# A 31-tap convolution beside projections: GpSimd's taps taken as products from ScalarE, twelve of them, and layer 0's mask and sinks loaded in the projection code

## Chip, cores and metric

One core of a Trainium2 chip. The metric is device microseconds of one execution; the kernel before has 3096.5 us, the median of three runs (3095.42 to 3097.85).

## What is computed

A backbone of two layers over 1024 latent tokens and 256 context tokens of width 1024. The change lies in layer 0. From the normalized, modulated input `h` one projection gives a gated pair for a convolution (2 x 512 columns), queries (512), keys and values (128 each):

```
def conformer_conv(z, conv_w, conv_b, ln_g, ln_b):
    val, gate = z[..., :CONV_A_DIM], z[..., CONV_A_DIM:]
    u = val * jax.nn.sigmoid(gate)
    u = dwconv(u, conv_w, conv_b, half, half)          # 31 taps per channel, 512 channels
    u = layer_norm(u, ln_g, ln_b)
    return jax.nn.silu(u)
...
    s_lat = jnp.where(valid[None, :, None, None], s_lat, NEG_INF)       # the window's mask
    sink_l = sink.astype(jnp.float32).reshape(1, 1, kvh, g, 1, 1)
    p_lat, p_ctx, _ = joint_softmax([s_lat, s_ctx, sink_l])
```

The convolution and the windowed attention stand side by side; their outputs are joined and projected.

## The kernel before

Activations lie with channels on partitions and tokens along the free axis, in groups of 512, 512 and 256 tokens (`TOK`). Every product is made three times, with a high and a low part of weight and input (`gemm`, L315 to L317, on TensorE); its result lies in one of four PSUM banks (`bank`, tile `mm`) until ACT or DVE evicts it. A weight block (`wcol`) is loaded by SP, its high part cast on ACT (L295) and its low part subtracted on DVE or POOL (L298).

At the start x and the context are loaded by SP (L570), transposed by PE (L579), copied out of PSUM by DVE and ACT in turn (L580), squared on ACT (L469) and summed on POOL (L473). From these sums come the root mean squares (L436 to L457), from the modulation vectors (L358, L345, L350, L411) the normalized input (L496 to L503), and then the first projection. Parameters go by small loads that ACT issues (L270); a tile `par` holds four groups of them until PE transposes each (L274).

`proj0` walks the list `PROJ0 = g0 g1 q0 g2 q1 g3 k q23`. `glu(i)` projects gate and value of channel block i and forms a tile `u` of 1325 columns in SBUF; it then spawns `conv(i, U)`, a generator that is advanced while later projections are written down (`pump`). `conv` takes tap 15 with the bias on ACT into `ca`, which lies in PSUM (L638); the first 8 other taps (`PTAPS`) on POOL, each as a product into a buffer `cp` (L645) and an addition of the sum so far (L647); the other 22 on DVE as multiply-adds into `ca` (L650). DVE joins both sums in `co` (L653), and SP writes that out. `qproj` projects queries (L780), `kvproj` keys and values (L706 evicts the values, L321 splits the keys, L709 and L710 rotate them). Beside them `mods` makes modulation vectors in the background: PE multiplies (L369), ACT copies the result `t` (L345), PE transposes it (L350), DVE adds the bias (L411). Then the queries' rotations (`qstack`, L746 to L762) and the values' transposes (`vstack`, L731).

`attn0` follows. It takes PSUM's banks of `ca` for the scores (`big`), loads mask and sink on ACT's queue (L801, L803) and negates the sink on DVE (L805). Scores are L861 and L868, the mask and the maximum L873, the exponential L878, the transposes of the weights L906.

What order the instructions of an engine stand in is set by a scheduler from the code's priorities and its own estimates, not by the code's order alone; on each engine they then run in that order. A DMA also waits until the load before it on its lane (there are eight) has landed.

Of the kernel before, what the change touches and what calls it, by code (L numbers as in the profile page):

```python
# [11 lines left out]
F32 = mybir.dt.float32  # L12
F32R = mybir.dt.float32r
AF = mybir.ActivationFunctionType
ALU = mybir.AluOpType
# [26 lines left out]
YF = 6.0  # L42
O0 = "G"
MS = ((0, 5), (1, 1), (1, 0), (1, 2), (1, 4), (1, 3), (1, 5)), ()
PTAPS = 8
WS = {"p0": P0W, "o0": O0, "f0": "GV", "c0": "GV", "p1": "GV", "m1": "G", "o1": "V", "f1": "G"}
PB0 = 4
LAG0 = 3
# [50 lines left out]
def tile_backbone(ctx: ExitStack, tc: tile.TileContext, a: dict, out: bass.AP):  # L99
    nc = tc.nc  # L100
    V, S, G, T = nc.vector, nc.scalar, nc.gpsimd, nc.tensor
# [21 lines left out]
    def nm(s):  # L123
        uid[0] += 1
        return f"{s}{uid[0]}"
# [135 lines left out]
    for r, items in enumerate(rows):  # L261
        n = 0
# [343 lines left out]
    CW, UW = SEQ + 15 + CTX, SEQ + 15 + CTX + 30  # L606
    COFF = (0, 512, SEQ + 15)

    def mixer0(hs, nxt, xs0):
        w = a["ab_w_in"][0]  # L610
        pc = ph[0]
        rcos, rsin = pc.tile([128, 1024], F32, name="rcos", bufs=1), pc.tile([128, 1024], F32, name="rsin", bufs=1)
        protr = pc.tile([128, 3, 128], F32R, name="protr", bufs=1)
        with tc.tile_pool(name="m0a", bufs=1) as pa:
            prep = proj0(hs, w, pa, rcos, rsin, protr, xs0)
        psum_side("big", 2)
        cat = Lazy()
        with tc.tile_pool(name="m0b", bufs=1) as pb:
            attn0(pb, *prep, cat)
        ws[0] = "o0"  # L620
        with tc.tile_pool(name="m0o", bufs=8 * len(YPO)) as po:
            for i, g in enumerate(GO0):
                if i < 2:
                    spawn(cat.load(GO0[i + 1]), "cat")
                ys, sq, last = outproj(a["ab_w_out"][0], cat, g, (lambda g: [po.tile([128, 512], F32, tag="y", name=nm("y")) for _ in range(8)]) if g in YPO else (lambda g: acts(g, 8, F32, "y")), lambda g: PO0[g], range(7, -1, -1) if g in OR0 else None)
                drain("cat")
                spawn(update(0, g, ys, sq, 2, last, True, (0, 3, 4) if g < 2 else None, nxt, PU0[g]))
            pumping[0] = True
            while not posted >= {(0, g) for g in YPO}:
                advance(flows["norm"])  # L630
            pumping[0] = False

    def proj0(hs, w, pa, rcos, rsin, protr, xs0):
        def conv(i, U):
            wc = lambda k: cols("acw", k * 4 + i)
            A = wide()[:, 0:CW]
            B = None
            S.activation(A, U[:, 15:15 + CW], AF.Identity, scale=wc(15), bias=cols("acb", i))  # L638
            taps = [k for k in range(31) if k != 15]
            pt, dt = taps[:PTAPS], taps[PTAPS:]  # L640
            nch = 6
            for c in range(nch):
                for k in pt[c::nch]:
                    P = pa.tile([128, CW], F32, tag="cp", name=nm("cp"), bufs=2)
                    G.tensor_scalar(P, U[:, k:k + CW], wc(k), 1.0, ALU.mult, ALU.mult)  # L645
                    if B is not None:
                        G.tensor_add(P, P, B)  # L647
                    B = P
                for k in dt[c::nch]:
                    V.scalar_tensor_tensor(A, U[:, k:k + CW], wc(k), A, ALU.mult, ALU.add)  # L650
                yield CY
            O = pa.tile([128, CW], F32, tag="co", name=nm("co"), bufs=2)
            V.tensor_add(O, A, B)  # L653
            for g in range(3):
                nc.sync.dma_start(cd[g][:, i], O[:, COFF[g]:COFF[g] + TOK[g]])

        st = pa.tile([128, CW], F32, tag="cp", name=nm("par"), bufs=2)
        for r in range(1, 5):
            spawn(params(r, st[:, r * 128 - 128:r * 128]), "par")

# [29 lines left out]
        def kvproj():  # L690
            prot = tmp(384).rearrange("p (a b) -> p a b", a=3)
            nc.scalar.dma_start(prot, a["rot"])
            V.tensor_copy(protr, prot)
            wk, wv = wcol(w, 1536), wcol(w, 1664)
            for g in range(3):
                n = TOK[g]
                ps = bank()[:, 0:n]
                gemm(ps, wk, *hs[g])
                if g < 2:
                    kh, kl = tmp(dt=F32R), tmp(dt=F32R)  # L700
                    split(ps, kh, kl)
                else:
                    V.tensor_copy(KFC[:, 0], ps)
                p2 = bank()[:, 0:n]
                gemm(p2, wv, *hs[g])
                S.copy(VF[:, OFF[g]:OFF[g] + n] if g < 2 else KFC[:, 1], p2)  # L706
                if g < 2:
                    pp = bank()
                    T.matmul(pp, protr[:, 0], kh, start=True, stop=False)  # L709
                    T.matmul(pp, protr[:, 0], kl, start=False, stop=True)  # L710
                    dst, m2 = KF[:, OFF[g]:OFF[g] + n], tmp()
                    V.tensor_mul(dst, ps, rcos[:, OFF[g]:OFF[g] + n])
                    V.tensor_mul(m2, pp, rsin[:, OFF[g]:OFF[g] + n])
                    V.tensor_add(dst, dst, m2)
# [50 lines left out]
        KH, qs = [], {}  # L765
# [30 lines left out]
        drain("bg")  # L796
        return KH[0:2], KH[2], vstack, kstack, qstack, qs

    def attn0(pc, KH, KC, vstack, kstack, qstack, qs, cat):
        msk = pc.tile([128, 1152], F32, name="msk")  # L800
        nc.scalar.dma_start(msk, a["win_mask"])  # L801
        sink = pc.tile([128, 8], F32, name="sink")
        nc.scalar.dma_start(sink, a["b_sink"].to_broadcast([128, 8]))  # L803
        nsink = pc.tile([128, 8], F32, name="nsink")
        V.tensor_scalar_mul(nsink, sink, -1.0)  # L805

        cath, catl = [[], [], []], [[], [], []]

# [38 lines left out]
        def scores(i, b, RAW, ROT, res):  # L847
            kv = i // 2
            pair = pc.tile([128, 1282], F32, tag="p", name=nm("p"), bufs=PB0).rearrange("p (j n) -> p j n", j=2)
            mx = pc.tile([128, 2], F32, tag="mx", name=nm("mx"), bufs=4)  # L850
            nmx = pc.tile([128, 2], F32, tag="nmx", name=nm("nmx"), bufs=4)
            den = pc.tile([128, 2], F32, tag="den", name=nm("den"), bufs=4)
            ss = []
            for j in range(2):
                s = bank2()
                if b < 8:
                    k0, k1 = max(0, b - 1), min(8, b + 2)
                    nw = 128 * (k1 - k0)
                    kt = list(range(k0, k1)) + [8, 9]
                    for x in range(2):  # L860
                        T.matmul(s[:, 512 - nw:512], ROT[j][:, b * 128:b * 128 + 128], KH[kv][x][:, k0 * 128:k1 * 128], start=x == 0, stop=x == 1)  # L861
                    q = RAW[j][0][:, b * 128:b * 128 + 128]
                    mk = msk[:, 0:640] if 0 < b < 7 else (msk[:, 128:640] if b == 0 else msk[:, 640:1152])
                else:
                    nw, kt, mk = 0, [8, 9], msk[:, 384:640]
                    q = RAW[j][1][:, (b - 8) * 128:(b - 8) * 128 + 128]
                for x in range(2):
                    T.matmul(s[:, 512:768], q, KC[:, kv, x], start=x == 0, stop=x == 1)  # L868
                n = nw + 256
                if j == 0:  # L870
                    gcopy(pair[:, :, n], sink[:, 2 * i:2 * i + 2])
                    res += [[pair[:, j] for j in range(2)], kt]
                V.tensor_tensor_reduce(out=pair[:, j, 0:n], in0=s[:, 512 - nw:768], in1=mk, op0=ALU.add, op1=ALU.max, scale=1.0, scalar=-3.0e38, accum_out=mx[:, j:j + 1])  # L873
                if j:
                    V.scalar_tensor_tensor(nmx, mx, -1.0, nsink[:, 2 * i:2 * i + 2], ALU.mult, ALU.min)
                yield
            for j in range(2):
                S.activation(pair[:, j, 0:n + 1], pair[:, j, 0:n + 1], AF.Exp, bias=nmx[:, j:j + 1], accum_out=den[:, j:j + 1])  # L878
                yield
            V.reciprocal(den, den)  # L880
            for j in range(2):
                norm1(N0[j], pair[:, j, 0:n], pair[:, j, 0:n], den[:, j:j + 1])
# [329 lines left out]
    def mla(pc, tab, KR, wv):  # L1212
# [163 lines left out]
        def head(h, g):  # L1376
            qh, ql, qc = (x[:, OFF[g]:OFF[g] + 512] for x in Q[h])
            kh, kl, kc = K[h % NK]
            po = psum["po"].tile([128, 512], F32, tag="po", name=nm("po"))
            P = []  # L1380

            def pv(t):
                v = VA[:, t, h // 2, h % 2:h % 2 + 2].rearrange("p b m -> p (b m)")
                T.matmul(po, v, P[t], start=t == 0, stop=t == 9)  # L1384

            for t in range(10):
# [13 lines left out]
                S.activation(p, st, AF.Exp, scale=scale)  # L1400
                P.append(p)
                if t % 2 and t > PVD:
# [298 lines left out]
    hs, nxt = Lazy(), Lazy()  # L1701
# [125 lines left out]
```

## Time and profile before

| | |
|---|---|
| median of three runs | 3096.5 us (3095.42 to 3097.85) |
| the profiled execution | 3100.69 us, its span 3098.9 us |
| mean granted TensorE clock | 0.974 of full speed |
| PE busy | 2942.0 us (95%) |
| DVE, ACT, POOL busy | 1747.0, 1093.4 and 990.6 us (56%, 35%, 32%) |

The span is what the trace shows; the execution's own time is 1.8 us longer, and that execution 4.2 us above the median. Busy shares are means over stages that differ: in layer 0's projections DVE and POOL are busy much more than over the span, so the stage is to be read by itself.

### The profile page before, as it was taken

To read this page: it belongs to the slowest core of one execution; us is meant where nothing else is said; L and a number is where in the kernel's file an instruction comes from. 1 tells how busy PE (TensorE), PEld (TensorE's weight loads), DVE (VectorE), ACT (ScalarE), POOL (GpSimd) and SP (SyncE) were. 2 spreads that over 40 slices of the span, in tenths; PEclk is the share of its full clock that TensorE was granted. 3 is DMA by queue.
4 is the path that set the end of the run, shared out by engine and by line. 5 is a ranking of instruction groups with operands and counts; after the bars stand their busy time and mean duration, and the time that the engine had idled before them with its cause. 6 is when DMAs were issued, how large, how long until landed. Compare 5 with 4: busy or idle time off the path is not lost. (4 is left out here: it accounts for less than half of the span.)

```text
span 3098.9 us, 37481 instructions
## 1 busy us (share of the span) xinstructions
PE 2942.0 (95%) x14441; PEld 2356.5 (76%) x14441; DVE 1747.0 (56%) x2631; ACT 1093.4 (35%) x1631; POOL 990.6 (32%) x730
## 2 busy tenths in 40 slices
PE   7997899899999999999999889999998999999998
PEld 4886777778888888889997556666686888888886
DVE  4799883665654455568545986667355132232234
ACT  4213884532221112145433763333344222111213
POOL 4676546821110011055432341110253222112223
PEclk8998999999999999999999899999998999999999
DMA  8343113434442344269744230010152121111212
GB/s 295 119 129 100 37 34 111 147 101 129 139 136 82 116 144 145 88 195 281 246 155 152 94 111 26 31 38 28 57 160 89 48 62 55 34 41 55 61 41 109
DMA packets 330768, 327.04 MB, mean 106 GB/s; under 512 B 27121, under 2 KB 280734, under 8 KB 330590
## 3 DMA queue, kind: packets, MB, share of 16 engines
q1 hardware_dynamic: 326784, 321.74, 32.3%
q10 hardware_dynamic: 3806, 2.91, 0.3%
q8 instruction: 113, 1.85, 0.2%
q14 instruction: 65, 0.53, 0.1%
HBM read 255.36 MB, written 69.21 MB: 105 GB/s over the span
## 5 line engine op out<-in xcount | busy, mean ns | idle before, releaser
L298 POOL TENSOR_TENSOR wl<-wr,wh 128x1024 fp32r<-128x1024 f32 x154 | 379.9, 2468 | 1314.2 <-ACT wh L295 1283.1
L295 ACT CAST wh<-wr 128x1024 fp32r<-128x1024 f32 x248 | 259.9, 1049 | 1072.3 <-PE big L316 682.3
L315 PE MATMUL big<-hh,wh 128*128 128x512 f32 x1376 | 541.2, 394 | 4.9 <-DVE ga L1485 2.6
L316 PE MATMUL big<-hl,wh 128*128 128x512 f32 x1376 | 538.6, 392 | 3.1 <-POOL hl L503 3.1
L317 PE MATMUL big<-hh,wl 128*128 128x512 f32 x1376 | 538.8, 392 | 0.6 <-DVE wl L298 0.6
L315 PE MATMUL mm<-hh,wh 128*128 128x256 f32 (+1 forms) x1000 | 346.0, 346 | 9.6 <-DVE i L1031 9.5
L316 PE MATMUL mm<-hl,wh 128*128 128x256 f32 (+1 forms) x1000 | 339.0, 339 | 4.0 <-POOL hl L503 2.0
L317 PE MATMUL mm<-hh,wl 128*128 128x256 f32 (+1 forms) x1000 | 338.0, 338 | 3.2 <-POOL wl L298 2.5
L315 PEld LDWEIGHTS big<-hh,wh 128*128 128x128 f32 x1376 | 260.7, 190 | 61.9 <-ACT hh L498 3.4
L316 PEld LDWEIGHTS big<-hl,wh 128*128 128x128 f32 x1376 | 260.4, 189 | 58.9 <-POOL hl L503 4.3
L317 PEld LDWEIGHTS big<-hh,wl 128*128 128x128 f32 x1376 | 260.5, 189 | 55.6 <-DVE wl L298 1.0
L1553 PE MATMUL mm<-zh,wh 128*128 128x512 f32 x704 | 276.6, 393 | 1.2 <-ACT xt L1656 0.7
L1554 PE MATMUL mm<-zl,wh 128*128 128x512 f32 x704 | 275.0, 391 | 0.3 <-DVE zl L322 0.3
L1555 PE MATMUL mm<-zh,wl 128*128 128x512 f32 x704 | 275.2, 391 | 0.0
L1560 DVE TENSOR_TENSOR acc<-acc,mm 128x512 f32<-128x512 f32 x224 | 150.5, 684 | 178.7 <-PE mm L1555 178.5
L473 POOL TENSOR_TENSOR sq<-t,sq 128x512 f32<-128x512 f32 (+1 forms) x153 | 194.8, 1276 | 170.2 <-ACT t L469 152.0
L1485 DVE SCALAR_TENSOR_TENSOR ga<-big,C,ga 128x1023 f32<-128x1023 f32 x86 | 110.2, 1281 | 235.1 <-ACT ga L1498 233.8
L315 PEld LDWEIGHTS mm<-hh,wh 128*128 128x128 f32 x1000 | 192.3, 192 | 35.7 <-DVE i L1031 9.9
L316 PEld LDWEIGHTS mm<-hl,wh 128*128 128x128 f32 x1000 | 191.9, 192 | 29.4 <-POOL hl L503 5.0
L317 PEld LDWEIGHTS mm<-hh,wl 128*128 128x128 f32 x1000 | 191.6, 192 | 24.3 <-POOL wl L298 3.3
L398 DVE SCALAR_TENSOR_TENSOR wa<-wm,sc,wa 128x256 f32<-128x256 f32 x280 | 148.9, 556 | 90.4 <-DMA wm<-in_w_mod_dram 87.6
L298 DVE TENSOR_TENSOR wl<-wr,wh 128x1024 fp32r<-128x1024 f32 x94 | 131.5, 1399 | 111.6 <-ACT wh L295 108.6
(350 smaller groups left out, 5278.5 us busy)
## 6 DMA issues: line engine op xcount, KB each, us to landing
wr<-in_ffn_w_up_dram SPq DMA_DIRECT2D x132, 512.0 KB, 4.3
wm<-in_w_mod_dram SPq DMA_DIRECT2D x224, 128.0 KB, 2.2
wr<-in_ffn_w_down_dram SPq DMA_DIRECT2D x44, 512.0 KB, 3.5
wm<-in_w_mod_dram SPq DMA_DIRECT2D x40, 512.0 KB, 6.5
xd<-x SPq DMA_DIRECT2D x38, 512.0 KB, 4.1
x<-xd SPq DMA_DIRECT2D x38, 512.0 KB, 6.6
wr<-in_ab_w_out_dram SPq DMA_DIRECT2D x24, 512.0 KB, 7.2
wdd<-wh SPq DMA_DIRECT2D x22, 512.0 KB, 2.6
```

What stands on the lines that cost most here:

```text
L295: S.copy(hi[:, 0:nk, 0:m], raw[:, 0:nk, 0:m])
L298: (G if e[wn[0] % len(e)] == "G" else V).tensor_sub(lo[:, 0:nk, 0:m], raw[:, 0:nk, 0:m], f32(hi[:, 0:nk, 0:m]))
L315: T.matmul(ps, wh, xh[k], start=i == 0, stop=False)
L316: T.matmul(ps, wh, xl[k], start=False, stop=False)
L317: T.matmul(ps, wl, xh[k], start=False, stop=i == n - 1)
L398: V.scalar_tensor_tensor(acc[:, v], raw, sc[:, k, v:v + 1], acc[:, v], ALU.mult, ALU.add)
L473: self.eng.tensor_add(self.acc[-1], t, self.acc[-1])
L1485: V.scalar_tensor_tensor(dst[:, lo:hi], src[:, lo + d - o:hi + d - o], k, dst[:, lo:hi], ALU.mult, ALU.add)
L1553: T.matmul(ps, wh, zh, start=j == j0, stop=False)
L1554: T.matmul(ps, wh, zl, start=False, stop=False)
L1555: T.matmul(ps, wl, zh, start=False, stop=j == j1 - 1)
L1560: V.tensor_add(ys[g][c], ys[g][c], ps)
```

## The change

The tap products move from POOL (`G.tensor_scalar`) to ACT (`S.mul`), POOL keeps the additions, and there are 12 such taps a block instead of 8, so DVE has 18 instead of 22. `cp` has three buffers instead of two, `co` one instead of two. The mask's first 640 columns, the sink and its negative get tiles that outlive the projections, and their loads stand in `kvproj`'s code; the last 512 columns (`msk7`) are loaded in `attn0`.

```diff
-PTAPS = 8
+PTAPS = 12
...
+        masks = [pc.tile([128, n], F32, name=s_, bufs=1) for s_, n in (("msk", 640), ("sink", 8), ("nsink", 8))]
...
-                    P = pa.tile([128, CW], F32, tag="cp", name=nm("cp"), bufs=2)
-                    G.tensor_scalar(P, U[:, k:k + CW], wc(k), 1.0, ALU.mult, ALU.mult)
+                    P = pa.tile([128, CW], F32, tag="cp", name=nm("cp"), bufs=3)
+                    S.mul(P, U[:, k:k + CW], wc(k))
                     if B is not None:
                         G.tensor_add(P, P, B)
...
-            O = pa.tile([128, CW], F32, tag="co", name=nm("co"), bufs=2)
+            O = pa.tile([128, CW], F32, tag="co", name=nm("co"), bufs=1)
...
-        st = pa.tile([128, CW], F32, tag="cp", name=nm("par"), bufs=2)
+        st = pa.tile([128, CW], F32, tag="cp", name=nm("par"), bufs=3)
...
             nc.scalar.dma_start(prot, a["rot"])
+            nc.scalar.dma_start(masks[0], a["win_mask"][:, 0:640])
+            nc.scalar.dma_start(masks[1], a["b_sink"].to_broadcast([128, 8]))
+            V.tensor_scalar_mul(masks[2], masks[1], -1.0)
...
-        msk = pc.tile([128, 1152], F32, name="msk")
-        nc.scalar.dma_start(msk, a["win_mask"])
-        sink = pc.tile([128, 8], F32, name="sink")
-        nc.scalar.dma_start(sink, a["b_sink"].to_broadcast([128, 8]))
-        nsink = pc.tile([128, 8], F32, name="nsink")
-        V.tensor_scalar_mul(nsink, sink, -1.0)
+        msk, sink, nsink = masks
+        msk7 = pc.tile([128, 512], F32, name="msk7")
+        nc.scalar.dma_start(msk7, a["win_mask"][:, 640:1152])
...
-                    mk = msk[:, 0:640] if 0 < b < 7 else (msk[:, 128:640] if b == 0 else msk[:, 640:1152])
+                    mk = msk[:, 0:640] if 0 < b < 7 else (msk[:, 128:640] if b == 0 else msk7)
```

With the change the lines below L611 have numbers higher by 1 to 4: the products are L646, the additions L648, the multiply-adds L651, `co` L654, the gate's eviction L676, the value's L710.

PE's order is the same but for some instructions at the first scores. The other engines' orders differ up to the first part of the attention and are the same behind it. Three places follow.

At the program's start, on ACT, behind the parameters' loads; `x` are the copies of the transposed input. Before:

```order
L270 DMA par_645<-in_ffn_conv_w_dram 66x128
L270 DMA par_645<-in_ffn_conv_b_dram 22x128
L580 COPY x_157<-mm_169 128x512
L580 COPY x_158<-mm_187 128x512
L469 ACTIVATE sq_167<-x_157 128x512
```

and with the change:

```order
L270 DMA par_648<-in_ffn_conv_w_dram 66x128
L270 DMA par_648<-in_ffn_conv_b_dram 22x128
L694 DMA msk<-in_win_mask_dram 128x640
L695 DMA sink<-in_b_sink_dram 128x8
L580 COPY x_157<-mm_169 128x512
L580 COPY x_158<-mm_187 128x512
L469 ACTIVATE sq_167<-x_157 128x512
```

The loads of mask and sink stand here, ahead of ACT's first copy of x. On DVE, at the same place (the piece of the difference):

```order
 L233 MEMSET ones 128x128
 L235 MEMSET eps_c 128x1
 L275 COPY C<-mm_93 128x128
+L696 TENSOR_SCALAR nsink<-sink 128x8
 L580 COPY x_157<-mm_161 128x512
 L580 COPY x_158<-mm_178 128x512
```

The sink's negation stands ahead of all of DVE's copies of x.

On ACT in the first convolution block, from `ca` of that block on; `u` are evictions of the gate, `t` of the modulation products. Before:

```order
L638 ACTIVATE ca_892<-u_649,C 128x1295
L675 ACTIVATE u_857<-mm_867 128x512
L675 ACTIVATE u_857<-mm_908 128x512
L345 COPY t_959<-mm_946 128x256
L295 CAST wh_1250<-wr_1248 128x1024
L675 ACTIVATE u_857<-mm_962 128x256
L345 COPY t_1044<-mm_1031 128x256
L295 CAST wh_1369<-wr_1367 128x1024
L345 COPY t_1161<-mm_1148 128x256
```

With the change the same stretch from the sixth product on (`cp_1028`), with the evictions `u_860<-mm_963` and `t_1047`, which is `t_1044` of before:

```order
L646 ACTIVATE cp_1028<-u_652,C 128x1295
L646 ACTIVATE cp_1075<-u_652,C 128x1295
L676 ACTIVATE u_860<-mm_963 128x256
L646 ACTIVATE cp_1078<-u_652,C 128x1295
L646 ACTIVATE cp_1147<-u_652,C 128x1295
L295 CAST wh_1261<-wr_1259 128x1024
L646 ACTIVATE cp_1150<-u_652,C 128x1295
L646 ACTIVATE cp_1199<-u_652,C 128x1295
L345 COPY t_1047<-mm_1034 128x256
L646 ACTIVATE cp_1202<-u_652,C 128x1295
L295 CAST wh_1378<-wr_1376 128x1024
```

Each eviction now has products ahead of it; `t_1047` stands behind the eleventh.

On ACT in the fourth block, where keys and values are projected; `vf` is the eviction of a value half, `t_1930` and `t_2030` (before `t_1908` and `t_2003`) that of a key half. Before:

```order
L345 COPY t_1860<-mm_1847 128x256
L692 DMA t_1863<-in_rot_dram 128x384
L321 CAST t_1908<-mm_1878 128x512
L706 COPY vf_648<-mm_1912 128x512
L345 COPY t_1957<-mm_1944 128x256
L638 ACTIVATE ca_2160<-u_1614,C 128x1295
L321 CAST t_2003<-mm_1967 128x512
```

With the change, from the fourth product of this block on:

```order
L646 ACTIVATE cp_2288<-u_1630,C 128x1295
L646 ACTIVATE cp_2342<-u_1630,C 128x1295
L646 ACTIVATE cp_2345<-u_1630,C 128x1295
L646 ACTIVATE cp_2438<-u_1630,C 128x1295
L710 COPY vf_651<-mm_1934 128x512
L345 COPY t_1981<-mm_1968 128x256
L646 ACTIVATE cp_2441<-u_1630,C 128x1295
L646 ACTIVATE cp_2447<-u_1630,C 128x1295
L646 ACTIVATE cp_2450<-u_1630,C 128x1295
L646 ACTIVATE cp_2456<-u_1630,C 128x1295
L646 ACTIVATE cp_2459<-u_1630,C 128x1295
L321 CAST t_2030<-mm_1991 128x512
```

The first value half's eviction now stands behind seven products, the second key half's behind all twelve.

## Rows read from the trace of the kernel before

**Rows 1.** Windows: us, busy us of each engine (instructions), clock, DMA share, GB/s.

```profile
80.00:270.00 190.00, 190.00 (x1120) 154.90 (x1119) 169.59 (x145) 43.77 (x72) 136.15 (x70) 1.00 0.38 119
...
300.00:320.00 20.00, 7.35 (x25) 6.68 (x26) 17.55 (x36) 7.33 (x14) 1.44 (x6) 0.50 0.51 159
...
320.00:460.00 140.00, 133.79 (x1216) 106.92 (x1215) 120.78 (x339) 120.64 (x262) 73.51 (x104) 1.00 0.09 29
```

**Rows 2.** Three lines of the convolution, whole span: ns min/median/max, first and last start.

```profile
L645 POOL TENSOR_SCALAR cp<-u,C x32: 1358/1363/2450, 98.6 to 267.4; 128x1295 f32<-128x1295 f32 x32
...
L647 POOL TENSOR_TENSOR cp<-cp,cp x28: 2959/2992/3982, 111.0 to 268.9; 128x1295 f32<-128x1295 f32 x28
...
L650 DVE SCALAR_TENSOR_TENSOR ca<-u,C,ca x88: 1554/1570/1574, 101.0 to 298.9; 128x1295 f32<-128x1295 f32 x88
```

**Rows 3.** ACT's groups by line and shape from 85 to 310 us: busy, mean ns | idle.

```profile
L638 ACT ACTIVATE ca<-u,C 128x1295 f32<-128x1295 f32 x4 | 5.7, 1433 | 5.4 <-DVE co L653 5.4
```

**Rows 4.** Timeline of ACT and its DMA issues, start: start us, us, instruction [idle before <-releaser].

```profile
5.14 0.26 ACTq L270 DMA_DIRECT2D par<-in_a_ln_g_dram  x1
...
8.74 0.32 ACTq L270 DMA_DIRECT2D par<-in_lru_gate_b_dram  x1
...
14.40 1.07 ACT L580 COPY x<-mm 128x512 f32<-128x512 f32 x2 [1.26 <-PE mm L579]
```

**Rows 5.** Timeline of SP's issues at the start; the loads of x, time to landing.

```profile
14.24 1.83 SPq L570 DMA_DIRECT2D xr<-in_ctx_dram  x2
...
DMA to landing us min/median/max: 4.6/4.9/6.4
```

**Rows 6.** Timeline of POOL from 10 to 42 us.

```profile
16.60 24.20 POOL L473 TENSOR_TENSOR sq<-t,sq 128x512 f32<-128x512 f32 x21 [14.81 <-ACT t L469]
```

**Rows 7.** Timeline of DVE and PE between there and the first projection.

```profile
38.42 1.49 DVE L345 COPY t<-mm 128x512 f32<-128x512 f32 x2 [8.88 <-POOL sq L473]
...
59.03 0.99 PE L315 MATMUL mm<-hh,wh 128*128 128x512 f32 x1
```

**Rows 8.** Timeline of ACT around the first convolution block.

```profile
98.85 1.43 ACT L638 ACTIVATE ca<-u,C 128x1295 f32<-128x1295 f32 x1
...
120.40 0.37 ACT L345 COPY t<-mm 128x256 f32<-128x256 f32 x1 [5.73 <-PE mm L369]
```

**Rows 9.** Timeline of PE at the second modulation product.

```profile
125.88 0.50 PE L350 MATMUL mm<-sel,t 128*128 128x2 f32 x4
```

**Rows 10.** Timeline of ACT around the fourth block.

```profile
224.13 0.37 ACT L345 COPY t<-mm 128x256 f32<-128x256 f32 x1 [0.42 <-PE mm L369]
...
235.50 0.59 ACT L706 COPY vf<-mm 128x512 f32<-128x512 f32 x1 [5.47 <-PE mm L317]
```

**Rows 11.** Timeline of PE in the key and value projections.

```profile
236.97 0.39 PE L315 MATMUL mm<-hh,wh 128*128 128x512 f32 x1
```

**Rows 12.** Timeline of PE from the queries' turn to the first transposes of the attention.

```profile
277.43 0.50 PE L751 MATMUL mm<-sraw,protr 128*128 128x512 f32 x1 [2.88 <-POOL sraw L747]
278.84 0.50 PE L752 MATMUL mm<-sraw,protr 128*128 128x512 f32 x1 [0.91 <-POOL sraw L747]
...
295.71 0.44 PE L731 MATMUL mm<-ident,kfc 128*128 128x128 f32 x2 [0.56 <-ACT t L780]
...
303.17 0.79 PE L861 MATMUL big<-k,srot 128*128 128x256 f32 x2 [7.02 <-DVE co L653]
...
320.71 1.03 PE L906 MATMUL mm<-ident,p 128*128 128x128 f32 x8
```

**Rows 13.** Windows around the pause before 278.84, columns as in rows 1.

```profile
280.00:283.00 3.00, 3.00 (x8) 2.31 (x8) 2.97 (x5) 0.00 (x0) 1.50 (x2) 0.50 0.01 4
283.00:284.00 1.00, 1.00 (x6) 0.78 (x5) 0.97 (x2) 0.00 (x0) 0.00 (x0) 0.99 0.38 128
```

**Rows 14.** Timeline of DVE at the seam.

```profile
313.45 0.68 DVE L873 CUSTOM_DVE_ANT_0 p<-big,msk 128x512 f32<-128x512 f32 x1
```

**Rows 15.** DVE's groups by line and shape from 320 to 460 us.

```profile
L398 DVE SCALAR_TENSOR_TENSOR wa<-wm,sc,wa 128x256 f32<-128x256 f32 x10 | 6.4, 644 | 0.0
```

More of the change, by code (lines that the diff above doesn't have):

```diff
@@ L613, in mixer0 @@
         protr = pc.tile([128, 3, 128], F32R, name="protr", bufs=1)
+        masks = [pc.tile([128, n], F32, name=s_, bufs=1) for s_, n in (("msk", 640), ("sink", 8), ("nsink", 8))]
         with tc.tile_pool(name="m0a", bufs=1) as pa:
-            prep = proj0(hs, w, pa, rcos, rsin, protr, xs0)
+            prep = proj0(hs, w, pa, rcos, rsin, protr, xs0, masks)
         psum_side("big", 2)
@@ L618, in mixer0 @@
         with tc.tile_pool(name="m0b", bufs=1) as pb:
-            attn0(pb, *prep, cat)
+            attn0(pb, *prep, cat, masks)
         ws[0] = "o0"
@@ L631, in mixer0, with proj0 @@
             pumping[0] = False
-    def proj0(hs, w, pa, rcos, rsin, protr, xs0):
+    def proj0(hs, w, pa, rcos, rsin, protr, xs0, masks):
         def conv(i, U):
@@ L797, in proj0, with attn0 @@
         return KH[0:2], KH[2], vstack, kstack, qstack, qs
-    def attn0(pc, KH, KC, vstack, kstack, qstack, qs, cat):
-        msk = pc.tile([128, 1152], F32, name="msk")
-        nc.scalar.dma_start(msk, a["win_mask"])
-        sink = pc.tile([128, 8], F32, name="sink")
-        nc.scalar.dma_start(sink, a["b_sink"].to_broadcast([128, 8]))
-        nsink = pc.tile([128, 8], F32, name="nsink")
-        V.tensor_scalar_mul(nsink, sink, -1.0)
+    def attn0(pc, KH, KC, vstack, kstack, qstack, qs, cat, masks):
+        msk, sink, nsink = masks
+        msk7 = pc.tile([128, 512], F32, name="msk7")
+        nc.scalar.dma_start(msk7, a["win_mask"][:, 640:1152])
         cath, catl = [[], [], []], [[], [], []]
```

## Prediction

> **What bounds the kernel now.** I read the stages first [rows 1]. From 80 to 270 us, while layer 0's input projections run, TensorE is busy 190.00 of 190.00 us at full clock: nothing there can be gained by relieving another engine, and every microsecond that PE is made to wait is added to the end. DVE is at 169.59 us in it, ACT at only 43.77. From 300 to 320 PE works 7.35 of 20 us, at a granted clock of 0.50: this seam between projections and attention is the one place where the change can win. From 320 to 460 PE has 133.79 of 140 us. The later order of every engine is unchanged, so what happens up to some 330 us is only carried along.
>
> The convolution's own rows [rows 2]: POOL makes 32 products of 1363 ns and 28 additions of 2992 ns (43.6 and 83.8 us), DVE 88 multiply-adds of 1570 ns (138 us). ACT's own instruction of that shape is the bias form, 1433 ns [rows 3].
>
> **The cost of each part.** *Moved taps.* DVE loses 16 multiply-adds, 16 x 1.57 = 25.1 us. POOL loses 32 x 1.36 = 43.6 us and gains 16 x 2.99 = 47.8: about even. ACT gains 48 products; none of before stands on ACT, the nearest row says 1.43 us each (another engine's row of the same work, 1.36, is the other bound), 65 to 69 us beside 43.77: enough room in sum. None of these sums is on PE's path before the seam, so there they are worth nothing in themselves.
>
> *Masks and sinks.* The code puts these loads into the key projection, but the changed order has them at the program's start: ACT issues msk and sink ahead of its first copy of x, and nsink stands on DVE ahead of every copy of x. So DVE waits for the sink to land. Its DMA waits in turn for its lane, freed by the sixth load of x; before, the second context load waits for the same landing and is issued by 16.07, so some 15.75 [rows 5]. A small load of that stretch holds its lane for 3.6 us (issued 5.14, the next on its lane 8.74 [rows 4]); the loads of x have a median of 4.9 [rows 5]. So the sink lands between 19.4 and 20.7. From ACT's copies to POOL's first sum of squares took 14.40 to 16.60 = 2.2 us [rows 4, 6], nsink about 0.2. POOL thus starts at 21.8 to 23.1 instead of 16.60, and is then busy for 24.20 us on end [rows 6], with DVE waiting 8.88 us for it at 38.42 [rows 7]: that chain leads to the first projection. **+5.2 us** (bounds 0, if the first copies are not the pace, and +6.5; the small load is the nearest row).
> The Trainium skill, on the page "DMA: Bandwidth & Descriptors" (Anatomy of one DMA), gives a DMA about 2.0 us of fixed cost; by that the sink would be there at some 17.8, and this term would be an estimated +3.6 instead of +5.2. The 3.6 us of this trace's own small load differs from it, and I go by the row.
>
> *The new wait on ACT.* There are three product buffers, each freed by an addition, so ACT can be at most two products ahead of POOL, which takes 2.99 plus about 0.09 us between instructions, 3.08 a tap. ACT is in order: evictions of PSUM that stand behind a waiting product wait with it. In block 0 (times as before, without the 5.2): the bias form at 98.85 [rows 8], products 1 and 2 to 103.1, their sum to 106.1; product 3 follows, its sum ends at 110.7, so product 4 runs to 112.2; the fifth, in the third buffer that the parameters held until then, to 114.2. From there the pace is POOL's: its sums end at about 118.2, 121.3, 124.4, 127.4 and 130.5, and the 11th product runs 130.5 to 131.9. Behind it stands the eviction of a modulation product, which ran at 120.40 [rows 8] and now ends at 132.3. PE wants it at 125.88 [rows 9]: **6.4 us** of stall, where before there were 5 us to spare. In block 3 the first two products stand behind the eviction of 224.13 [rows 10] and end at 227.3; sums end at 230.4, 233.5, 236.6 and 239.6, the seventh product at 241.1, and behind it stands the eviction of the first value half (235.50 before [rows 10], now done 241.8). PE needs that bank for the key half that began at 236.97 [rows 11]: **5.2 us**. The five products after it have no eviction between them; the last ends near 256.5, the key half's eviction behind it at 257.1, where PE with its 5.2 us would be at about 253.5 to 254.3: **3.7 us**. The same walk through blocks 1 and 2 gives 2.1 and 3.7 us, less certain. Sum 6.4 + 2.1 + 3.7 + 5.2 + 3.7 = 21.1 us; I take **+20.6** with bounds of 10 (the middle ones hidden, the others a half less) and 25.
>
> *Clock.* After the pause that ends at 278.84 the granted clock was 0.50 in 280 to 283 and 0.99 from 283 [rows 12, 13]: some 3.4 us at half pace, 1.7 us lost. Two of the five new pauses are longer than that one by far or near; **+3.4** (bounds 0 and 6.8).
>
> *Gains.* PE's waits for POOL's raw queries, 2.88 and 0.91 us [rows 12], go, since DVE and POOL are done with the convolution earlier against PE; with that pause's clock loss **-5.5**. At the seam, the last transpose of the projections at 295.71 to the first of the attention at 320.71 [rows 12] is 25 us, in which scores wait for the last co (7.02, at 303.17) and the next for DVE (mx at 313.45 [rows 14]). With 25 us less on DVE, and the projections some 20 us longer, neither is late. From that mx to the transposes are 7.3 us that remain, and scores ahead of it some 4: 25 becomes about 12, **-13** (bounds -8 and -15). What is late next there is DVE's background weighting (10 instructions of 644 ns left in the attention [rows 15]), part of which now runs before: **-3** at most -5, at least 0, since PE is nearly full there.
>
> Sum: 5.2 + 20.6 + 3.4 - 5.5 - 13 - 3 = **+7.7 us**. The profiled execution took 3100.7 us, 4.2 above the median of the three runs; the sum is of its terms and would make it 3108.4, and the median 3096.5 + 7.7 = **3104.2 us**.
>
> **Rivals.** Without the stalls and their clock the sum is 5.2 - 5.5 - 13 - 3 = -16.3 us, so the stalls decide the sign: above 16.3 us it is slower than before, below 10.1 faster by more than 0.2%.
> (A) *ACT holds PE much less, and it is faster*: a stall that PE takes in block 0 lets POOL and ACT catch up for every later place, so that 6 to 10 us remain, none long enough to cost clock: -16.3 + 8 = -8.3, 3088. For it: ACT's own work is only a third of the stage. Against: the products do not wait for ACT's time but for 11 sums of 3.08 us in order, and blocks 0 and 3 have their places at the chain's end. Between A and my case, with 10 to 17 us, lies no change that can be told, about 3094.
> (B) *ACT delays more*: stalls 25, clock 6.8, the seam only -8 because late evictions push DVE's queue too: 6 + 25 + 6.8 - 5.5 - 8 - 3 = +21, 3118. For it: the walk leaves out DVE's part in an eviction. Against: DVE has 20 us more for 25 less work.
> (C) *The early sink costs nothing*, because the first copies of x are not the pace: 7.7 - 5.2 = +2.5, 3099. Against: POOL's unbroken 24.20 us [rows 6].
> (D) *The change does not do what it says*: its loads indeed stand elsewhere than in the key projection; if attention then waits at the seam as before and the products never hold PE, both sides vanish, 3096.
>
> **How the numbers follow.** A difference under 0.2% (6.2 us: 3090.3 to 3102.7) can't be told from none. My case has 0.45, with its own range 3099 to 3113, a quarter of it inside 0.2%; A 0.20, between A and mine 0.12, B 0.12, C 0.06 (half inside 0.2%), D 0.05. Slower: 0.34 + 0.12 + 0.03 = 0.49; same: 0.11 + 0.12 + 0.03 + 0.05 = 0.31; faster: 0.20. The range that leaves out no more than 2 in 10 goes from A's better half, 3086, to B's middle, 3118.
>
> **What would show it.** The first projection 4 to 6 us later than at 59.03 [rows 7], DVE waiting for the sink's DMA; products on ACT of 1.3 to 1.45 us spaced by some 3.1; PE waits for ACT's t and vf of 2 to 6 us between 130 and 285 where there was none; the raw query waits gone; 10 to 14 us instead of 25 at the seam. I am wrong if PE stays at full share between 85 and 270 (A), if DVE still ends last at the seam (B), or if the first projection has not moved (C).

## The result, and the profile after

The changed kernel takes 3126.7 us (median of four runs, 3121.8 to 3129.6) against 3097.2 us before: the ratio is 1.0089, with a 95% interval of 1.0076 to 1.0102, so it is some 28 us slower. The prediction said slower, by 7.7 us, and its range ended at 3118: the sign was right and the size was not. The profiled execution has a span of 3123.4 us, 24.5 more than that of before; that is less than 28, because the profiled execution of before was one of its longer ones. This is where the 24.5 us come from:

| | before | after | difference |
|---|---|---|---|
| first projection begins | 59.03 | 63.29 | +4.3 |
| from there to the last transposes of the projections | 236.7 | 261.9 | +25.2 |
| from those to the first transposes of the attention | 25.0 | 19.0 | -6.0 |
| from those to the end | 2778.2 | 2779.1 | +0.9 |

The start, first on ACT (the sink is issued at 15.39), then on DVE, POOL and PE, in timelines whose columns are start, duration, instruction and the idle time before it:

```profile
15.39 0.36 ACTq L695 DMA_DIRECT2D sink<-in_b_sink_dram  x1
15.79 1.07 ACT L580 COPY x<-mm 128x512 f32<-128x512 f32 x2 [3.30 <-DMA par<-in_ffn_conv_w_dram]
22.12 0.63 ACT L469 ACTIVATE sq<-x 128x512 f32<-128x512 f32 x1 [5.26 <-DVE x L580]
```

```profile
21.33 0.17 DVE L696 TENSOR_SCALAR nsink<-sink 128x8 f32<-128x8 f32 x1 [14.14 <-DMA sink<-in_b_sink_dram]
21.41 1.88 DVE L580 COPY x<-mm 128x512 f32<-128x512 f32 x3
```

```profile
23.36 24.18 POOL L473 TENSOR_TENSOR sq<-t,sq 128x512 f32<-128x512 f32 x21 [21.57 <-ACT t L469]
```

```profile
63.29 0.51 PE L315 MATMUL mm<-hh,wh 128*128 128x512 f32 x1 [0.65 <-ACT hh L498]
```

The sink takes 5.9 us from its issue to nsink (5.1 to 5.9 to its landing in the four kernels that load it here); ACT's copies are done before, but its squares wait 5.26 us for DVE's copy. POOL's sums begin at 23.36 and again run without a pause [rows 6].

The products and the additions, each by its line: duration min/median/max, and how long the engine stood idle before them for whom (us, times):

```profile
L646 ACT ACTIVATE cp<-u,C x48: 1361/1376/1382, 105.9 to 283.0; 128x1295 f32<-128x1295 f32 x48
...
  POOL cp L648: 56.3, 34
```

```profile
L648 POOL TENSOR_TENSOR cp<-cp,cp x44: 2914/2982/3894, 108.6 to 286.0; 128x1295 f32<-128x1295 f32 x44
...
  ACT cp L646: 49.8, 7
```

ACT does a product in 1376 ns, but stands 56.3 us in front of products, 34 times, waiting for an addition on POOL; POOL's own pace is 2982 ns, as before [rows 2]. What that does to an eviction, on ACT and on PE in block 0 (compare [rows 8, 9]):

```profile
132.89 1.38 ACT L646 ACTIVATE cp<-u,C 128x1295 f32<-128x1295 f32 x1 [0.78 <-POOL cp L648]
136.75 1.37 ACT L646 ACTIVATE cp<-u,C 128x1295 f32<-128x1295 f32 x1 [2.48 <-POOL cp L648]
138.03 0.35 ACT L345 COPY t<-mm 128x256 f32<-128x256 f32 x1
```

```profile
138.44 1.01 PE L350 MATMUL mm<-sel,t 128*128 128x2 f32 x4 [6.03 <-ACT t L345]
```

The two products ahead of t are 3.9 us apart, and PE waits 6.03 us for it. The next longest wait of this kind is in block 2:

```profile
222.34 1.01 PE L350 MATMUL mm<-sel,t 128*128 128x2 f32 x4 [5.77 <-ACT t L345]
```

PE's waits from 88 us to the scores, by line and releaser (us in total, times, longest); before there were none until 272:

```profile
PE mm L350 <- ACT t L345: 15.0, 5, 6.0
PE mm L315 <- ACT vf L710: 3.8, 1, 3.8
PE mm L714 <- DVE t L322: 1.1, 2, 0.9
PE mm L713 <- ACT t L321: 0.9, 1, 0.9
```

That is 20.8 us in sum, 19.7 of them for ACT. And the stretches in which the granted clock was at its lower level after these waits (windows, columns as in [rows 1]):

```profile
136.00:144.00 8.00, 5.56 (x27) 5.56 (x28) 5.54 (x5) 3.01 (x3) 7.76 (x4) 0.57 0.13 38
...
218.00:229.00 11.00, 6.66 (x18) 5.41 (x19) 6.88 (x6) 5.70 (x7) 10.76 (x4) 0.53 0.45 139
...
266.00:274.00 8.00, 4.72 (x13) 3.75 (x14) 7.96 (x7) 4.06 (x5) 7.76 (x4) 0.57 0.21 74
...
287.00:291.00 4.00, 4.00 (x23) 4.00 (x22) 3.96 (x4) 0.28 (x1) 1.99 (x1) 0.58 0.23 80
```

Busy time times the share of the clock that is missing is an estimate of what PE lost: 2.4 + 3.1 + 2.0 + 1.7 = 9.2 us. Before it was 1.7 in this part [rows 13].

The seam between projections and attention: PE before at its second wait, PE with the change, and DVE with the change:

```profile
314.19 1.01 PE L861 MATMUL big<-k,srot 128*128 128x384 f32 x2 [8.95 <-DVE mx L873]
```

```profile
325.22 0.44 PE L735 MATMUL mm<-ident,kfc 128*128 128x128 f32 x2
325.41 0.48 PE L862 MATMUL big<-k,srot 128*128 128x256 f32 x2
...
335.69 1.01 PE L862 MATMUL big<-k,srot 128*128 128x384 f32 x2 [9.08 <-DVE mx L874]
...
344.26 1.12 PE L907 MATMUL mm<-ident,p 128*128 128x128 f32 x4 [2.21 <-ACT p L223]
```

```profile
315.56 2.64 DVE L398 SCALAR_TENSOR_TENSOR wa<-wm,sc,wa 128x256 f32<-128x256 f32 x4 [2.18 <-DMA wm<-in_w_mod_dram]
...
323.27 6.20 DVE L398 SCALAR_TENSOR_TENSOR wa<-wm,sc,wa 128x256 f32<-128x256 f32 x5
330.94 0.88 DVE L398 SCALAR_TENSOR_TENSOR wa<-wm,sc,wa 128x256 f32<-128x256 f32 x2 [1.47 <-DMA wm<-in_w_mod_dram]
332.94 0.88 DVE L398 SCALAR_TENSOR_TENSOR wa<-wm,sc,wa 128x256 f32<-128x256 f32 x2 [1.12 <-DMA wm<-in_w_mod_dram]
...
334.94 0.68 DVE L874 CUSTOM_DVE_ANT_0 p<-big,msk 128x512 f32<-128x512 f32 x1
```

The scores begin 0.2 us after the projections' last transposes instead of 7.5 [rows 12], but the next ones wait 9.08 us for the first maximum, which DVE does at 334.94. Before they waited as long, 8.95 us, then behind the end of the convolution and the rotations on DVE. So of two waits at the seam the change took away the first and kept the second: from 312 us on, sixteen instructions of the weighting `wa` (a background task of the next stage) stand ahead of the maximum, and they wait for their weights' DMAs. Before, there were four.

### The profile page after: what moved, and what is told of

It reads as the page before. It is cut to its first block, busy times and chain, and to the rows that moved or that the text cites. A ratio compares the mean times of both kernels' runs of the same rounds, so it can differ in the third digit from the quotient of the medians.

```text
span 3123.4 us, 37518 instructions
## 1 busy us (share of the span) xinstructions
PE 2946.9 (94%) x14441; PEld 2362.8 (76%) x14441; DVE 1730.0 (55%) x2615; ACT 1155.8 (37%) x1679; POOL 991.8 (32%) x714
```

## The experiments

Each kernel was run beside the kernel before on the same chip. The time of the kernel before differs a little between them (3097 to 3101 us), so ratios are what is compared; 0.001 is 3.1 us. A difference of two ratios is uncertain by some 0.002, or 6 us.

**The mask loads ordered later.** The loads on ACT's queue get an ordering after the fourth block's gate eviction; all else stands as in the change.

```diff
+        last_ev = [None]
...
-                ev = S.activation(U[:, 15 + COFF[g]:15 + COFF[g] + TOK[g]], ps, AF.Sigmoid)
+                ev = last_ev[0] = S.activation(U[:, 15 + COFF[g]:15 + COFF[g] + TOK[g]], ps, AF.Sigmoid)
...
-            nc.scalar.dma_start(masks[0], a["win_mask"][:, 0:640])
-            nc.scalar.dma_start(masks[1], a["b_sink"].to_broadcast([128, 8]))
+            gate(nc.scalar.dma_start(masks[0], a["win_mask"][:, 0:640]), last_ev[0])
+            gate(nc.scalar.dma_start(masks[1], a["b_sink"].to_broadcast([128, 8])), last_ev[0])
```

> The change, with the loads of msk and sink ordered behind the fourth block's last gate eviction on ACT, so that nsink leaves the program's start; nothing else moves but these instructions. Theory (two separate costs: an early sink that DVE waits for, and products that hold up evictions on ACT): DVE's first copies are back at 11 to 14 us, the first projection at 59 instead of 63.3, and the time 4 to 7 us below the change, 3119 to 3123; the waits of PE for ACT between 110 and 290 us stay at about 20 us. Rival (the early loads disturb more than the start, by delayed weights and clock): 15 us or more come back, 3112 or less. Second rival (the start is hidden): no difference, 3126.

Ratio 1.0061 (1.0046 to 1.0076), 0.0028 or some 9 us below the change. DVE's first copy of x, PE's first projection, and PE's waits until the scores:

```profile
11.00 0.69 DVE L580 COPY x<-mm 128x512 f32<-128x512 f32 x1 [3.84 <-PE mm L579]
```

```profile
57.30 0.51 PE L315 MATMUL mm<-hh,wh 128*128 128x512 f32 x1 [0.65 <-ACT hh L498]
```

```profile
PE mm L350 <- ACT t L345: 14.9, 5, 6.0
PE mm L315 <- ACT vf L712: 3.8, 1, 3.8
```

DVE copies x at 11.00 again, and the projections begin 6 us earlier. PE's waits are what they were to a tenth. So the two costs are separate. The first, 9 us by these ratios, can't be told from the theory's 4 to 7.

**The mask part taken back.** `attn0` loads mask and sink as in the kernel before; the products on ACT stay.

```diff
-        msk, sink, nsink = masks
-        msk7 = pc.tile([128, 512], F32, name="msk7")
+        msk = pc.tile([128, 1152], F32, name="msk")
+        nc.scalar.dma_start(msk, a["win_mask"])
...
+        V.tensor_scalar_mul(nsink, sink, -1.0)
...
```

> The change without its mask part: msk, sink and nsink loaded at the start of the attention as before, the products on ACT kept. Theory: the start as in the run with the ordered loads (first projection at 59), the stalls for ACT still about 20 us, and at the seam no loss, as DVE's first mask instruction comes late for another reason there; 3119 to 3124. Rival (the mask part is worth something at the seam): 3 us or more above the run with the ordered loads.

Ratio 1.0064 (1.0049 to 1.0079), the first projection at 56.81, PE's waits 12.7 us for t and 3.8 for vf. That is the run above within its interval, and the theory's time: loading the mask early buys nothing that can be measured here. It also gives the price of the moved taps alone, with what they win at the seam already taken off: 0.0064, some 20 us.

**The mask part alone**, on the kernel before with its 8 taps as products on POOL. Against the change:

```diff
-PTAPS = 12
+PTAPS = 8
...
-                    P = pa.tile([128, CW], F32, tag="cp", name=nm("cp"), bufs=3)
-                    S.mul(P, U[:, k:k + CW], wc(k))
+                    P = pa.tile([128, CW], F32, tag="cp", name=nm("cp"), bufs=2)
+                    G.tensor_scalar(P, U[:, k:k + CW], wc(k), 1.0, ALU.mult, ALU.mult)
...
```

> The kernel before with the change's mask part alone: 8 taps with products on POOL, msk, sink and nsink as in the change, where they come first at the program's start. Theory (nsink holds DVE's first copies until the sink lands): the first projection 5 to 8 us later than in the run with the ordered loads (57.3), nothing regained in the projections, where PE is full; the seam may give 1 to 3 us back; the time 3 to 8 us above before. Rival (the start costs only beside the products' stalls): no difference from before.

Ratio 1.0018 (1.0009 to 1.0027), some 6 us. nsink on DVE and the first projection:

```profile
21.91 0.17 DVE L696 TENSOR_SCALAR nsink<-sink 128x8 f32<-128x8 f32 x1 [14.62 <-DMA sink<-in_b_sink_dram]
```

```profile
66.45 0.99 PE L315 MATMUL mm<-hh,wh 128*128 128x512 f32 x1
```

The price is that of the start, with no products on ACT. The time is in the theory's range; the first projection is 9 us later than in the run with the ordered loads, more than the theory's 5 to 8. Over all runs the first projection begins at 57.6 us on the mean where the sink is loaded late (ten kernels, 56.2 to 59.0) and at 65.1 where it is first (four, 63.3 to 66.5): 7.5 us, with the profiled execution of the change the mildest case.

**Four product buffers.** The joined sum is written over the last one, which makes room.

```diff
-                    P = pa.tile([128, CW], F32, tag="cp", name=nm("cp"), bufs=3)
+                    P = pa.tile([128, CW], F32, tag="cp", name=nm("cp"), bufs=4)
...
-            O = pa.tile([128, CW], F32, tag="co", name=nm("co"), bufs=1)
+            O = B
...
```

> The change with four product buffers instead of three (the joined sum is written over the last one, so that co is not needed and SBUF holds it); PE's order is the same. Theory (ACT waits for POOL's additions through the buffers, one more buffer lets each product go about one addition, 3.08 us, earlier): each of the stalls of 6.0, 1.2, 1.6, 5.8, 3.8, 0.9 and 0.9 us gets about 3 us shorter, 20 become 6 to 9, the clock loss between 86 and 296 us falls from 9.6 to 3 to 5, and the time to 3105 to 3112. Rival (it is the amount of work on ACT, 48 products of 1.38 us, that delays the evictions, not the wait for buffers): stalls of 15 us or more remain, 3120 or more.

Ratio 1.0062 (1.0045 to 1.0078), 3121 us, 8 us below the change: the expectation fell, and both numbers of the rival (waits of 15 us or more, 3120 us or more) came true. PE's longer waits on ACT, and ACT's order in block 0:

```profile
PE mm L350 <- ACT t L345: 11.3, 3, 4.8
PE mm L713 <- ACT t L321: 2.9, 1, 2.9
```

```profile
121.86 1.38 ACT L646 ACTIVATE cp<-u,C 128x1295 f32<-128x1295 f32 x1 [1.66 <-POOL cp L648]
123.14 0.58 ACT L676 ACTIVATE u<-mm 128x512 f32<-128x512 f32 x1
123.62 0.36 ACT L345 COPY t<-mm 128x256 f32<-128x256 f32 x1
```

PE's waits in sum fall to 16.6 us, not to 6 to 9, and the clock loss to 6.8, not to 3 to 5. The scheduler used the free buffer to put two products more ahead of the first t (seven instead of five), so the gain of a buffer is spent on a longer queue: that place now costs 3.9 us where it cost 0.4, and the one behind it (6.0) is gone. As the order moved with the buffers, this run does not tell the wait for buffers from the amount of work on ACT; the run without additions below does.

**The evictions on DVE.** t and vf go to the engine that has lost 25 us of taps.

```diff
-            (S.copy if pool else V.tensor_copy)(t, ps)
+            V.tensor_copy(t, ps)
...
-                S.copy(VF[:, OFF[g]:OFF[g] + n] if g < 2 else KFC[:, 1], p2)
+                V.tensor_copy(VF[:, OFF[g]:OFF[g] + n] if g < 2 else KFC[:, 1], p2)
```

> The change with the modulation products' evictions (t) and the values' (vf) on DVE instead of ACT. Theory (evictions behind waiting products on ACT are what PE waits for): the waits for t and vf on ACT, 18.8 us, are gone; DVE's queue may add up to 1.6 us at each of some 15 places, of which PE has most to spare; the time 3100 to 3110. Rival (PE would wait for the same work wherever it is evicted, since DVE is as full): waits of the same size move to DVE, 3120 or more.

Ratio 1.0085 (1.0070 to 1.0100), 3128 us: no gain. The expectation fell. PE's waits, the three largest groups:

```profile
PE mm L315 <- ACT t L784: 9.7, 2, 6.8
PE mm L713 <- ACT t L321: 5.7, 1, 5.7
PE mm L350 <- DVE t L345: 4.3, 2, 4.1
```

Two thirds of the waits are now for the queries' evictions and the keys' parts, which also stand on ACT behind products. The time is the rival's, its reason is not: it expected DVE's queue to hold PE, and DVE has 4.3 and 1.8 us of the waits. PE walks from one of ACT's evictions to the next, and ACT's queue moves at the pace of the sums; whichever eviction is taken off it, the next one holds PE.

**The additions left out.** Ordered mask loads, and the 44 additions on POOL are not made, so that only a block's last product reaches its sum: the kernel computes something else and serves to measure alone. PE's, DVE's and SP's orders are those of the first run, ACT's differs by a few rows, and ACT does its 48 products. The edit beside that of the first run:

```diff
                     S.mul(P, U[:, k:k + CW], wc(k))
-                    if B is not None:
-                        G.tensor_add(P, P, B)
                     B = P
```

> The change with the ordered mask loads (as the first of these runs), and POOL's 44 additions of products left out, so that only the last product of each block reaches the sum; PE's, DVE's and SP's orders are the same, ACT's differs by a few rows. Theory (products wait on ACT for POOL's additions at 3.08 us a tap, and evictions behind them): with nothing to wait for ACT does a product in 1.38 us, the 20.8 us of PE's waits between 86 us and the first scores fall to 4 or less and the clock loss there from 9.7 to 3 or less; about 25 us less up to the first scores than in the run with additions, and 3095 to 3102 in all, as DVE is again as late as the projections. Rival (ACT's own 66 us of products are in the way): waits of 12 us or more remain, 3112 or more.

Ratio 0.9951 (0.9936 to 0.9965), 34 us below the run with the additions and 15 below the kernel before. The products' line, a window from 86 us to the end of the projections, and PE at the seam:

```profile
L646 ACT ACTIVATE cp<-u,C x48: 1357/1368/1387, 98.7 to 240.3; 128x1295 f32<-128x1295 f32 x48
...
  DVE u L684: 0.4, 1
```

```profile
86.00:285.00 199.00, 199.00 (x1175) 163.24 (x1175) 162.11 (x151) 104.38 (x118) 14.19 (x18) 1.00 0.42 131
```

```profile
297.38 1.01 PE L862 MATMUL big<-k,srot 128*128 128x384 f32 x2 [9.96 <-DVE mx L874]
```

ACT waits 0.4 us in front of all products, and PE is busy 199.00 of 199.00 us at full clock. ACT works 104 us in it and holds nobody up. The time is lower than even the theory had it (3095 to 3102); the seam has no part in that, as PE waits 9.96 us for the first maximum there, no less than in the change. This settles the projections: PE does not wait for the amount of work on ACT, it waits because ACT waits for POOL's sums. What it does not give is the price of POOL's work by itself, since POOL has only 14.19 us of work left in this stretch, nor that of the clock, whose loss goes together with the waits.

**Eight taps as products on ACT.** Ordered mask loads (the edit of the first run) and PTAPS = 8.

```diff
-PTAPS = 12
+PTAPS = 8
```

> The change with the ordered mask loads and 8 instead of 12 taps a block as products on ACT (32 products, 28 additions, 88 multiply-adds). Theory: a block's chain of sums is 7 x 3.08 = 22 us instead of 34, so evictions stand behind fewer products; the waits before the scores fall from 20.8 to 3 to 8 us, the clock loss to 4 or less, DVE has its 25 us again and ends near the scores as before; 3096 to 3106. Rival (any products on ACT hold PE as long): 3115 or more.

Ratio 1.0048 (1.0031 to 1.0064), 3116 us: the expectation fell, and the time is the rival's. PE still waits 14.1 us for ACT before the scores, not 3 to 8, and 12.1 us for the last co, where it waited 7.0 in the kernel before. POOL in block 1:

```profile
146.81 2.92 POOL L648 TENSOR_TENSOR cp<-cp,cp 128x1295 f32<-128x1295 f32 x1 [1.49 <-ACT cp L646]
151.21 2.95 POOL L648 TENSOR_TENSOR cp<-cp,cp 128x1295 f32<-128x1295 f32 x1 [1.49 <-ACT cp L646]
```

An addition every 4.4 us, each after a wait of 1.49 for its product, while the product waited 2.3 to 3.1 for the addition: the two engines take turns, which is no faster than POOL doing both (1.36 + 2.99). In block 1 they do so until 158, some 11 us after the co of block 0 (147.2); only then two products go in a row. A finished sum that holds the third buffer would do this, but no run tests that, and co is done well before. Fewer taps alone do not take the waits away.

**The weighting later.** Ordered mask loads, and the first two weight loads of the background task are ordered after the attention's first exponential.

```diff
+    first_exp = [None]
...
-            nc.sync.dma_start(raw, a["w_mod"][l, k * 128:k * 128 + 128, idx * D + n * w:idx * D + n * w + w])
+            gate(nc.sync.dma_start(raw, a["w_mod"][l, k * 128:k * 128 + 128, idx * D + n * w:idx * D + n * w + w]), first_exp[0] if (l, idx) == (0, 5) and i < 2 else None)
...
-                S.activation(pair[:, j, 0:n + 1], pair[:, j, 0:n + 1], AF.Exp, bias=nmx[:, j:j + 1], accum_out=den[:, j:j + 1])
+                ex = S.activation(pair[:, j, 0:n + 1], pair[:, j, 0:n + 1], AF.Exp, bias=nmx[:, j:j + 1], accum_out=den[:, j:j + 1])
+                first_exp[0] = first_exp[0] or ex
```

> The change with the ordered mask loads, and the first loads of the weights for the background modulation of the second half of layer 0 (the weighting wa on DVE) ordered behind the attention's first exponential, so that DVE's first masks and maxima don't stand behind some fourteen of them. Theory (at the seam DVE waits for these loads, and the scores for DVE): from the first scores to the first transposes 9 to 12 us instead of 19.7, the time 6 to 9 us below the run with the ordered mask loads, 3112 to 3116. Rival (the weighting costs the same wherever it runs): no difference, 3119 to 3123.

Ratio 1.0036 (1.0024 to 1.0048), some 8 us below the first run, as the theory had it. PE and DVE at the seam:

```profile
317.97 0.48 PE L866 MATMUL big<-k,srot 128*128 128x256 f32 x2
...
327.90 1.12 PE L912 MATMUL mm<-ident,p 128*128 128x128 f32 x4 [2.81 <-ACT p L223]
```

```profile
318.73 0.69 DVE L878 CUSTOM_DVE_ANT_0 p<-big,msk 128x512 f32<-128x512 f32 x1 [1.01 <-PE big L873]
```

From the scores to the transposes 9.9 us instead of 18.9 in the change; DVE's first maximum now waits for PE, and not PE for it. The seam's gain that the prediction counted on is there once these instructions are out of the way.

**Ten taps on POOL**, products there too, with ordered mask loads and later weighting (their edits as above). Against the kernel before:

```diff
-PTAPS = 8
+PTAPS = 10
```

> The kernel before, products on POOL, with 10 instead of 8 taps a block on POOL (88 becomes 80 multiply-adds on DVE), the ordered mask loads and the later weighting. Theory: ACT has no products, so PE has no waits in the projections; POOL's chain is 10 x 4.45 = 45 us of a block of about 46; DVE loses 12.5 us, so the scores begin 6 to 12 us earlier; 3085 to 3095. Rival (POOL is the pace of the last block): co later than before, 3100 or more.

Ratio 1.0015 (1.0005 to 1.0024), 3106 us: the rival's time, though not in the last block. DVE at the first co, and PE behind it:

```profile
150.76 1.51 DVE L656 TENSOR_TENSOR co<-ca,cp 128x1295 f32<-128x1295 f32 x1 [11.62 <-POOL cp L650]
```

```profile
152.39 0.80 PE L315 MATMUL mm<-hh,wh 128*128 128x512 f32 x1 [7.73 <-DVE MOD L413]
```

It is block 0 whose sum POOL ends late: co waits 11.62 us for it, and PE waits 7.73 us for a modulation vector that stands behind co on DVE. No other co of this run waits for POOL.

**The mends on the kernel before, and on the change.** The later weighting alone on the kernel before; the same with the ordered mask loads; and the change with ordered loads, four buffers and later weighting. The edits are those above.

> The kernel before with only the background weighting (wa on DVE) ordered behind the attention's first exponential; masks, taps and products as before. Theory: at its seam only two of the weighting's instructions and their waits stand ahead of the first maximum, so 2 to 4 us come back: 0.1% below before. Rival: nothing or a loss, as the weighting is pushed into an attention that has little room.

> The kernel before, 8 taps with products on POOL, with the change's mask part but its loads ordered behind the fourth block's gate eviction, and the later weighting. Theory: neither the early sink nor waits for ACT are there, and the seam has no mask load and fewer instructions ahead of the first maximum: 3 to 6 us below before, the fastest of these kernels that compute everything. Rival: DVE's 88 multiply-adds end the seam anyway, within 0.1% of before.

> The change (12 taps as products on ACT) with all three mends: ordered mask loads, four product buffers, the later weighting. Theory: the savings add, 8 us of the start, some 6 to 8 of the buffers and 8 to 10 of the seam: within 4 us of before, 3097 to 3105. Rival (with the stalls shorter DVE or POOL ends the seam again, so that they do not add): 3108 or more.

The first has 0.9992 (0.9983 to 1.0001), the second 0.9991 (0.9982 to 1.0000): 3 us, at the edge of what can be told, and the best that computes everything. The third has 1.0026 (1.0015 to 1.0036); the theory asked for 3097 to 3105, the rival for 3108 or more, and it has 3107.6. There the seam is as short as in the run with the later weighting (9.9 us), but PE's waits are close to those of the run with four buffers, 15.5 us and 7.8 of clock.

## Why the prediction was wrong in size

- **The early sink, +5.2: right.** The chain (sink, nsink, DVE's copies, ACT's squares, POOL's sums without a pause) is what the trace shows. The size lies within what the runs tell: 4.3 us in the profiled execution, 7.5 on the mean of the first projections, some 6 and 9 by the ratios. The sink's own part was too small, 3.6 us taken and 5.9 measured; POOL's sums began 6.8 us later and not 5.2. The Trainium skill's 2.0 us ("DMA: Bandwidth & Descriptors", Anatomy of one DMA) stand in a section on DMAs that GpSimd issues, and ACT issues this one; the measurement decides.
- **PE's waits behind ACT, +20.6: right in mechanism and sum, by luck so near.** 15.0 + 3.8 + 1.1 + 0.9 = 20.8 us, against 21.1 walked. Of the places, 6.4 was 6.03 with 0.4 at the t ahead of it; 2.1 and 3.7 were 2.7 (two waits) and 5.8; 5.2 was 3.8; 3.7 was 0.9 (its own sum, 257.1 less 253.5 to 254.3, gives 2.8 to 3.6). Another 1.1 us were waits for DVE, which the walk did not have. The errors of the places cancel. The run without additions shows the cause as the step put it.
- **Clock, +3.4: this step failed.** It priced two pauses at 1.7 us each, taken from the one pause of [rows 13]. There were four low stretches, 9.2 us lost in sum. In three of them the clock fell while PE was still waiting (the waits of 6.03, 5.77 and 3.77 us), and PE then worked on at the lower level for some 5, 6.7 and 4 us, against 3.4 before; the fourth followed two short waits of 0.9 and 0.2 us and lost 1.7. Another 2.4 us more than before were lost between 60 and 86 us, but the nine runs without the early sink lose 2.7 to 4.6 there, against 2.2 before, so this is not put down to the change.
- **The raw query waits, -5.5: right,** they are gone.
- **The seam, -13, and the attention, -3: these steps failed.** The seam gave 6.0, and the stretch behind it took 0.9 more. The step held that with 25 us less on DVE neither of the seam's two waits would be late. The first, for the last co (7.02 us before), is gone; the second, for DVE's first maximum, is 9.08 us where it was 8.95. The step did say that what is late next there is the weighting, but booked it as a gain, since part of it "now runs before". It counted the instructions' 644 ns and neither the DMAs that they wait for nor that DVE works in order: run before, they stand ahead of the first maximum. The run with the later weighting gave back 8 us. In the attention the ten weighting instructions (6.4 us on DVE [rows 15]) are indeed gone, and over the rest of the kernel PE gained nothing by it; before, it waited for DVE there 4.6 us in all, in eight waits of at most 1.6.
- The rivals: A (catching up) did not happen; the run with the additions left out shows what it would have needed. B (ACT delays more) was nearest, 3118, and the prediction had named its sign, DVE still last at the seam, which came true. But its reasons were longer stalls and evictions that push DVE's queue; the stalls were not longer, and it was the clock and the weighting. C and D are out: the first projection moved, and the products hold PE.

Clock 9.2 instead of 3.4, the seam 6 instead of 13, the attention 0.9 instead of -3 make 16.7 of the 16.8 us between the sum, 7.7, and the two spans' 24.5. The rest cancels: 2.4 us of clock at the first projections, against 1.8 us of waits for query evictions that were there before the last transposes and are gone, which the sum did not count, and 0.9 us less at the start.

## What to carry to other kernels

Work that is moved to an idle engine is not free if each piece waits for a slower engine through a small ring of buffers: the idle engine's queue then runs at the slow one's pace, and everything else that stands in it, PSUM evictions above all, with it. Look for what stands behind a wait in the same queue, not at the busy share. A scheduler that may hoist a load or a background task can put it ahead of the critical instruction of an in-order engine, as it did here twice; read the order, and give such work a place.

## What was not expected of the hardware

A load of 4 KB took 5.9 us at the start, in the company of the large loads of x (4.6 to 6.4 before [rows 5]) and with the mask's 320 KB issued 1.7 us ahead of it on the same queue, where a small load of the same stretch had held its lane for 3.6. Which of the two neighbours it is, no run separates. And PE's clock, once fallen to its lower level (0.50, 1.2 GHz) in the wait of 5.77 us, stayed there for all of the next 6.66 us of work (218 to 229) without a pause between, against 3.4 us after the pause of before.
